# Norm factors and the scaling of the first banks issued first in a decoder trunk of twelve sub-layers

## The chip, the cores and the metric

One NeuronCore of one Trainium2 chip runs the whole program in one launch. The metric is the device time of that launch in microseconds (us). The engines are TensorE (PE, matrix products into PSUM banks), VectorE (DVE), ScalarE (ACT), GpSimd (POOL) and SyncE (SP, here the queue that issues nearly all loads). Each engine runs its own queue of instructions, and semaphores tie the queues together.

## The reference

A trunk of four layers on 256 tokens of width 1024 in 32-bit floats. Each layer is x += 1/2 gate SwiGLU(h), x += gate mixer(h), x += 1/2 gate SwiGLU(h), so there are twelve sub-layers. The mixers are differential attention in layers 0 and 3, RWKV-7 in layer 1 and sliding-window attention in layer 2. Ahead of each sub-layer stands the same norm with modulation:

```
def rms_norm(x, g, eps=NORM_EPS):
    y = xf * lax.rsqrt(jnp.mean(xf * xf, axis=-1, keepdims=True) + eps)
    return (y * g.astype(jnp.float32)).astype(x.dtype)

mod = (cond @ ada_w[i] + ada_b[i])[:, None, :]
h = modulate(rms_norm(x, norm_g[i, 0]), sh1, sc1)        # h * (1 + scale) + shift
x = x + 0.5 * g1 * swiglu(h, ffn_w_in[i, 0], ffn_w_out[i, 0])
```

Queries and keys in both attentions, the outputs of the differential heads and the keys and outputs of the RWKV heads are normed too.

## The kernel before

The activations lie transposed, as eight tiles of 128 features by 256 tokens. PE multiplies in a split form: each operand is a pair, a rounded part `hi` and the rest `lo`, and one product is three matmuls (`mm3`, lines 287 to 289: hi by hi, hi by lo, lo by hi). Weights come from memory as `raw` slabs of 1 MB; ACT makes `hi` (line 269) and DVE makes `lo` (line 271), four pieces of 512 columns each for a slab. The activations of a sub-layer are pairs from the pool `hp` (tag `h`, 10 tiles).

**The order of work.** The program text says what depends on what. A planner then lays the instructions of each engine in one queue: it plays the program through with its own estimates, and whenever an engine is free it takes, among the instructions that are ready at that moment, the one that stands first in the program. A load is asked for some units before its use, so the casts of later weights stand early in the text. Each tile takes one of the buffers of its tag and waits while none is free.

**A norm.** `residual` (line 577) makes a new tile of x. `stat_add` squares it, and one matmul with ones sums the squares. `rsqrt` turns the sums into the factor by bit arithmetic and two steps of refinement: a transpose (393), one affine step (402), nine tiny DVE steps on 128 x 8 elements (409 and 411 to 418), and a transpose back (424). Each needs the one before. With `later=True` it returns the last transpose as a function `fin`, to be called when the caller wants it.

**The start of a sub-layer.** While the factor is not known, PE already multiplies the raw x: `pre` makes a pair `xh` of x times (1 + scale) times the norm's gain (lines 489 and 490), with the shift as two extra columns. `first_units` runs the first products on these pairs into banks a, d and b of a feed-forward sub-layer (a, b and c in a mixer). `make_h` then makes the eight true `h` pairs: `xr` (511, DVE), the hi part (513, ACT), the lo part (514, DVE). The first banks are put right afterwards by `unraw`: ACT copies the extra column (540), and DVE multiplies the bank by the factor (541), which is the last read of that bank but for the copy, so that the bank comes free. In the text `unraw` stands behind `make_h`. In a feed-forward sub-layer the next products on `h` go to bank d and bank a again. Loads of the second pair of column blocks stand behind `make_h` in the text, and the products for later modulation vectors (`ada_unit`, line 344, DVE) from the third pair on.

**The mixers.** A differential head norms query and key (`qknorm`) and later its output (line 947 and after); an RWKV tile norms the key (at line 1252) and its output (at line 1429), and lines 1441 to 1443 use the latter factor; line 1443 is the last read of a bank d that line 1391 of the next tile needs. These calls of `rsqrt` use `later=True`, with pauses between the two halves in which other heads or tiles are stepped. `split` makes pairs of the `h` tag in the RWKV layer.

Of the kernel before, what the change touches and what calls it, by code (L numbers as in the profile page):

```python
# [16 lines left out]
ALU = mybir.AluOpType  # L17
# [4 lines left out]
T = 256  # L22
# [206 lines left out]
class Trunk:  # L229
    def __init__(self, tc, ctx, aps, plan):  # L230
        self.tc, self.nc, self.A, self.plan = tc, tc.nc, aps, plan
        e = ctx.enter_context
        self.cst = e(tc.tile_pool(name="cst", bufs=1))
        self.xp = e(tc.tile_pool(name="xp", bufs=9))
        self.sm = e(tc.tile_pool(name="sm", bufs=2))
        self.nrm = e(tc.tile_pool(name="nrm", bufs=2))
        self.hp = e(tc.tile_pool(name="hp", bufs=10))
        self.sl = e(tc.tile_pool(name="sl", bufs=4))
        self.pp = e(tc.tile_pool(name="pp", bufs=2, space=bass.MemoryType.PSUM))
        self.adp = None  # L240
        self.uid = 0
# [140 lines left out]
        return self.mods[(l, m)]  # L382


    def rsqrt(self, ps, n, scale, eps, pool, floor=None, later=False, more=None):


        nc = self.nc
        w, nk = n * 32, n
        n += 0 if more is None else more.shape[1]  # L390
        if nk:
            t = pool.tile([P, w], F32, tag=f"rsq{nk}", name=self.n("rsqt"))
            nc.vector.transpose(t, ps)
        m_ = self.sm.tile([P, n], F32, tag=f"rm{n}", bufs=3, name=self.n("rm"))
        m = m_[:, :nk]
        if more is not None:
            nc.vector.tensor_scalar(m_[:, nk:], more, scale, eps, op0=ALU.mult, op1=ALU.add)
        g = nc.vector
        if nk:
            first = t.rearrange("p (j q) -> p j q", q=32)[:, :, 0]  # L400
            if floor is None:
                g.tensor_scalar(m, first, scale, eps, op0=ALU.mult, op1=ALU.add)
            else:
                g.tensor_scalar(m, first, scale, floor, op0=ALU.mult, op1=ALU.max)
        m = m_
        y = self.sm.tile([P, n], F32, tag=f"ry{n}", bufs=3, name=self.n("ry"))
        z = self.sm.tile([P, n], F32, tag=f"ru{n}", bufs=3, name=self.n("rz"))
        f = self.sm.tile([P, n], F32, tag=f"rf{n}", bufs=3, name=self.n("rf"))
        g.tensor_scalar(y.bitcast(I32), m.bitcast(I32), -0.5, float(0x5f3759df), op0=ALU.mult, op1=ALU.add)

        g.tensor_tensor(z, y, y, op=ALU.mult)
        g.tensor_tensor(z, z, m, op=ALU.mult)
        g.scalar_tensor_tensor(y, z, -3.0, y, op0=ALU.add, op1=ALU.mult)
        g.tensor_tensor(z, y, y, op=ALU.mult)
        g.tensor_tensor(z, z, m, op=ALU.mult)
        g.tensor_scalar(f, z, -0.1875 / 16, 0.625 / 4, op0=ALU.mult, op1=ALU.add)
        g.tensor_tensor(f, f, z, op=ALU.mult)
        g.scalar_tensor_tensor(y, f, -0.9375, y, op0=ALU.add, op1=ALU.mult)

        def fin():  # L420
            if not nk:
                return None, y
            r = pool.tile([P, w], F32, tag=f"rsq{nk}", name=self.n("rsq"))
            nc.vector.transpose(r, y[:, :nk].unsqueeze(2).to_broadcast([P, nk, 32]))
            return r if more is None else (r, y[:, nk:])

        return fin if later else fin()

    def stat_begin(self):
        self.ssum = None  # L430
# [105 lines left out]
    def unraw(self, bank, out, tag="ub"):  # L536

        nc = self.nc
        b = self.sm.tile([P, 1], F32, tag=tag, bufs=4, name=self.n(tag))
        nc.scalar.copy(b, bank[:, T:T + 1])  # L540
        nc.vector.tensor_tensor(out, bank[:, :T], self.rs, op=ALU.mult)  # L541
        return b

    def split(self, pool, tag, bufs, src, sbuf=True):
# [566 lines left out]
    def rwkv(self, l):  # L1111
        nc, A = self.nc, self.A
        self.t1 = 4
        with ExitStack() as c0:
# [8 lines left out]
            with ExitStack() as c:  # L1123
# [21 lines left out]
                def mixed(i, d):  # L1145
                    t = ap.tile([P, T], F32, tag="mix", bufs=4, name=self.n("mix"))
                    om = omu[:, i * 8 + d:i * 8 + d + 1]
                    if i < 3:
                        nc.scalar.activation(t, pt[:, d, 1:], AF.Identity, scale=om, bias=sh[:, d:d + 1])
                    else:  # L1150
                        nc.gpsimd.tensor_scalar(t, pt[:, d, 1:], om, sh[:, d:d + 1], op0=ALU.mult, op1=ALU.add)
                    nc.vector.scalar_tensor_tensor(t, pt[:, d, :T], self.v("mu", i * 8 + d), t, op0=ALU.mult,
                                                   op1=ALU.add)
                    return t

                rkv = []
                for i in range(3):
                    ms = []
                    for d in range(ND):
                        if i == 0:  # L1160
                            nc.vector.scalar_tensor_tensor(pt[:, d, 1:], self.x[d], a[:, d:d + 1], r, op0=ALU.mult,
                                                           op1=ALU.mult)
                        ms.append(self.split(self.hp, "h", 10, mixed(i, d)))
                    if i == 2:
                        break
                    dst = self.slab(("hi", "lo")[i], (P, ND, T))
                    rkv.append(dst)
                    for u in range(4):
                        w = unit(i * 4 + u)
                        bank = self.ps("a" if u % 2 == 0 else "d")  # L1170
                        self.project(w, 2, ms, [bank[:, :T], bank[:, T:]], korder=(u < 2))
                        nc.scalar.copy(dst[:, 2 * u:2 * u + 2], bank.rearrange("p (d t) -> p d t", d=2))
                        self.pump(l, 20)
                    if i == 0:
                        l1 = self.slab("raw")
                        nc.sync.dma_start(l1, A["rwl1"])
                        l1b = ap.tile([P, T], F32, name=self.n("l1b"))
                        nc.sync.dma_start(l1b, A["rwl1b"])
                        nc.sync.dma_start(lw2[:, 0], A["rwl2"][0:128, :])
                        nc.sync.dma_start(lw2[:, 1], A["rwl2"][128:256, :])  # L1180
                        nc.sync.dma_start(lw2[:, 2], A["rwl2"][256:384, :])
                        l1 = l1.rearrange("p (k c) -> p k c", k=ND)
                        l1b = l1b.rearrange("p (k c) -> p k c", k=ND)
                        pl = [self.ps("c"), self.ps("c"), self.ps("b"), self.ps("b")]
                        for d in range(ND):
                            f = dict(start=(d == 0), stop=(d == ND - 1))
                            m = mixed(3, d)
                            nc.tensor.matmul(pl[0][0:64, :T], l1[:, d, 0:64], m, **f)
                            m = mixed(4, d)
                            nc.tensor.matmul(pl[1][64:128, :T], l1[:, d, 64:128], m, **f)  # L1190
                            m = mixed(5, d)
                            nc.tensor.matmul(pl[2][:, :T], l1[:, d, 128:256], m, **f)
                            nc.tensor.matmul(pl[3][0:32, :T], l1b[:, d], m, **f)
                        nc.scalar.activation(lr[0:64, 0], pl[0][0:64, :T], AF.Tanh)
                        nc.scalar.copy(lr[64:128, 1], pl[1][64:128, :T])
                        nc.scalar.activation(lr[:, 2], pl[2][:, :T], AF.Tanh, scale=0.5)
                        nc.vector.tensor_scalar(lr[:, 2], lr[:, 2], 0.5, 0.5, op0=ALU.mult, op1=ALU.add)
                        nc.scalar.activation(lr[0:32, 3], pl[3][0:32, :T], AF.Tanh, scale=0.5)
                        nc.vector.tensor_scalar(lr[0:32, 3], lr[0:32, 3], 0.5, 0.5, op0=ALU.mult, op1=ALU.add)
# [3 lines left out]
    def rw_core(self, c, l, rkv, lw2, lr, hw, ms, unit):  # L1203
# [3 lines left out]
        nc, A = self.nc, self.A  # L1207
# [10 lines left out]
        outs = []  # L1218
# [9 lines left out]
        def tile_gen(d):  # L1228
# [25 lines left out]
            fin = self.rsqrt(st[:, :T], 8, 64.0, 0.0, bp, floor=1e-24, later=True)  # L1254
# [49 lines left out]
            for h in range(2):  # L1304
                nc.vector.tensor_tensor(zb[hd[h]], zu[hd[h], :, h, 0], id64[hd[h]].unsqueeze(1).to_broadcast([64, 4, 64]),
                                        op=ALU.add)
# [21 lines left out]
            b = [self.ps(inv), self.ps(inv)]  # L1328
# [38 lines left out]
            for t in range(2):  # L1367
                for hh in range(2):
                    for h in range(2):
                        i, u = t * 2 + hh, hh * 2 + t  # L1370
# [46 lines left out]
            oo = f1("oo", 2)  # L1417
# [12 lines left out]
            fin = self.rsqrt(pv[:, :T], 8, 1.0, 64e-5, bp, later=True)  # L1430
# [10 lines left out]
            nc.vector.scalar_tensor_tensor(oo, oo, self.v("lnxg", d), rn, op0=ALU.mult, op1=ALU.mult)  # L1441
            nc.vector.scalar_tensor_tensor(oo, oo, self.v("lnxb", d), tt, op0=ALU.add, op1=ALU.add)
            nc.vector.tensor_tensor(oo, oo, pb[:, T:], op=ALU.mult)
            outs.append(self.split(self.hp, "h", 10, oo))

        rkv.append(self.slab("raw", (P, ND, T)))

# [67 lines left out]
```

## Time and profile before

| what | value |
|---|---|
| median of 3 runs | 2309.99 us (2307.81 to 2311.01) |
| the profiled execution | 2310.26 us, its span 2308.4 us |
| PE busy | 2193.9 us (95%) |
| DVE busy | 1766.9 us (77%) |
| ACT busy | 1196.4 us (52%) |
| mean granted TensorE clock | 0.974 |

The span runs from the first to the last instruction of the program; 1.9 us of the profiled execution lie around it. Busy time counts an instruction from start to end, so neighbours on DVE overlap by up to a tenth of a microsecond. [...]

### The profile page before, as it was taken

To read this page: it belongs to the slowest core of one execution; us is meant where nothing else is said; L and a number is where in the kernel's file an instruction comes from. 1 tells how busy PE (TensorE), PEld (TensorE's weight loads), DVE (VectorE), ACT (ScalarE), POOL (GpSimd) and SP (SyncE) were. 2 spreads that over 40 slices of the span, in tenths; PEclk is the share of its full clock that TensorE was granted. 3 is DMA by queue.
4 is the path that set the end of the run, shared out by engine and by line. 5 is a ranking of instruction groups with operands and counts; after the bars stand their busy time and mean duration, and the time that the engine had idled before them with its cause. 6 is when DMAs were issued, how large, how long until landed. Compare 5 with 4: busy or idle time off the path is not lost.

```text
span 2308.4 us, 47699 instructions
## 1 busy us (share of the span) xinstructions
PE 2193.9 (95%) x19244; PEld 2104.0 (91%) x19244; DVE 1766.9 (77%) x4001; ACT 1196.4 (52%) x2675; POOL 112.7 (5%) x213
## 2 busy tenths in 40 slices
PE   7999899999999899888999999999999999999999
PEld 6999898999999687677999899888999999889999
DVE  6877999888855776767888965778889855999653
ACT  3545766445444474445444644586445444766442
POOL 0001001001000300001000100101001000101000
PEclk8999999999999998899999999999999999999999
DMA  8885456887754420026788665436888755554552
GB/s 341 357 330 207 176 190 243 341 328 289 277 183 183 148 74 2 21 74 239 285 317 329 261 249 183 157 146 231 338 321 305 282 183 183 185 190 158 201 183 74
DMA packets 72365, 505.90 MB, mean 219 GB/s; under 512 B 8016, under 2 KB 10448, under 8 KB 11600
## 3 DMA queue, kind: packets, MB, share of 16 engines
q1 hardware_dynamic: 71568, 502.20, 57.6%
q8 instruction: 151, 2.47, 0.4%
q10 hardware_dynamic: 576, 0.66, 0.1%
q14 instruction: 70, 0.57, 0.1%
HBM read 501.78 MB, written 1.05 MB: 218 GB/s over the span
## 4 chain that ended last, share of the span: by engine, by line
PE 45%; DVE 5%; ACT 1%; issue 1%; POOL 0%; DVEq 0%; ACTq 0%; POOLq 0%
PE psa L287 4%; PE psa L289 4%; PE psa L288 4%; PE psd L287 4%; PE psd L289 4%; PE psd L288 4%; PE psb L288 3%; PE psb L287 3%; PE psb L289 3%; PE psc L288 2%; PE psc L289 2%; PE psc L287 2%; DVE lo L271 2%; DVE x L577 1%; DVE xh L490 1%
## 5 line engine op out<-in xcount | busy, mean ns | idle before, releaser
L269 ACT CAST hi<-raw 128x512 fp32r<-128x512 f32 x1306 | 731.3, 618 | 720.2 <-issue 553.5
L271 DVE TENSOR_TENSOR lo<-raw,hi 128x512 fp32r<-128x512 f32 x1306 | 847.3, 691 | 240.2 <-ACT hi L269 239.3
L287 PE MATMUL psa<-h,hi 128*128 128x256 f32 x1336 | 377.7, 283 | 29.3 <-DVE sil L541 23.8
L289 PE MATMUL psa<-h,lo 128*128 128x256 f32 x1336 | 377.3, 282 | 0.0
L288 PE MATMUL psa<-h,hi 128*128 128x256 f32 x1336 | 376.8, 282 | 0.0
L287 PE MATMUL psd<-h,hi 128*128 128x256 f32 x1256 | 359.0, 286 | 0.0
L289 PE MATMUL psd<-h,lo 128*128 128x256 f32 x1256 | 359.0, 286 | 0.0
L288 PE MATMUL psd<-h,hi 128*128 128x256 f32 x1256 | 358.4, 285 | 0.0
L344 DVE SCALAR_TENSOR_TENSOR ada<-ada,cb 128x1024 f32<-128x1024 f32 x232 | 276.3, 1219 | 27.1 <-DMA ada<-in_ada_dram 27.1
L287 PEld LDWEIGHTS psa<-h,hi 128*128 128x128 f32 x1336 | 255.0, 191 | 31.1 <-ACT hi L269 17.3
L288 PEld LDWEIGHTS psa<-h,hi 128*128 128x128 f32 x1336 | 253.0, 189 | 0.2
L289 PEld LDWEIGHTS psa<-h,lo 128*128 128x128 f32 x1336 | 252.9, 189 | 0.0
L287 PEld LDWEIGHTS psd<-h,hi 128*128 128x128 f32 x1256 | 243.7, 194 | 0.7
L288 PEld LDWEIGHTS psd<-h,hi 128*128 128x128 f32 x1256 | 242.4, 193 | 0.7 <-issue 0.7
L289 PEld LDWEIGHTS psd<-h,lo 128*128 128x128 f32 x1256 | 242.0, 193 | 0.3
L289 PE MATMUL psb<-g,lo 128*128 128x256 f32 x704 | 199.3, 283 | 0.0
L287 PE MATMUL psb<-g,hi 128*128 128x256 f32 x704 | 199.3, 283 | 0.0
L288 PE MATMUL psb<-g,hi 128*128 128x256 f32 x704 | 199.2, 283 | 0.0
L288 PE MATMUL psc<-g,hi 128*128 128x256 f32 x704 | 199.0, 283 | 0.0
L289 PE MATMUL psc<-g,lo 128*128 128x256 f32 x704 | 199.0, 283 | 0.0
L287 PE MATMUL psc<-g,hi 128*128 128x256 f32 x704 | 198.9, 283 | 0.0
L289 PEld LDWEIGHTS psb<-g,lo 128*128 128x128 f32 x704 | 135.0, 192 | 0.0
(373 smaller groups left out, 4464.4 us busy)
## 6 DMA issues: line engine op xcount, KB each, us to landing
raw<-in_ffi_dram SPq DMA_DIRECT2D x175, 1024.0 KB, 4.9
ada<-in_ada_dram SPq DMA_DIRECT2D x116, 1024.0 KB, 7.3
raw<-in_ffo_dram SPq DMA_DIRECT2D x88, 1024.0 KB, 4.9
raw<-in_ada_dram SPq DMA_DIRECT2D x24, 1024.0 KB, 4.8
raw<-in_daqk_dram SPq DMA_DIRECT2D x16, 1024.0 KB, 4.8
raw<-in_rwr_dram SPq DMA_DIRECT2D x12, 1024.0 KB, 4.8
raw<-in_ff_dram SPq DMA_DIRECT2D x8, 1024.0 KB, 9.6
raw<-in_dav_dram SPq DMA_DIRECT2D x8, 1024.0 KB, 4.8
```

The source lines that it names most:

```text
L269: nc.scalar.copy(hi[:, sl], raw[:, sl])
L271: eng.tensor_tensor(lo[:, sl], raw[:, sl], hi[:, sl].bitcast(F32), op=ALU.subtract)
L287: nc.tensor.matmul(out, whi, ahi, start=start, stop=False, skip_group_check=True)
L288: nc.tensor.matmul(out, whi, alo, start=False, stop=False, skip_group_check=True)
L289: nc.tensor.matmul(out, wlo, ahi, start=False, stop=stop, skip_group_check=True)
L344: nc.vector.scalar_tensor_tensor(wk, wk, 1.0, self.cond, op0=ALU.mult, op1=ALU.mult, accum_out=raw[:, k:k + 1])
L490: nc.vector.scalar_tensor_tensor(h[:, 1, :T], self.x[d], a[:, d:d + 1], h[:, 0, :T].bitcast(F32), op0=ALU.mult, op1=ALU.subtract)
L577: nc.vector.scalar_tensor_tensor(t, acc[d // 2][:, (d % 2) * T:(d % 2 + 1) * T], gate[:, d:d + 1], self.x[d], op0=ALU.mult, op1=ALU.add)
```

## The change

`rsqrt` becomes a wrapper around the old body, now `_rsqrt`. Both halves, the steps down to line 418 and the transpose back, are traced inside `high_priority()`, which makes the planner treat the instructions traced inside as if they stood at the start of the program. The same is done to the two instructions of `unraw`. Dependences are as they were, and no instruction is added or removed. The pool `hp` gets 12 tiles in place of 10.

```
-        self.hp = e(tc.tile_pool(name="hp", bufs=10))
+        self.hp = e(tc.tile_pool(name="hp", bufs=12))
...
-    def rsqrt(self, ps, n, scale, eps, pool, floor=None, later=False, more=None):
+    def rsqrt(self, *args, later=False, **kw):
+
+        with self.tc.high_priority():
+            fin = self._rsqrt(*args, **kw)
+
+        def done():
+            with self.tc.high_priority():
+                return fin()
+
+        return done if later else done()
+
+    def _rsqrt(self, ps, n, scale, eps, pool, floor=None, more=None):
...
-        return fin if later else fin()
+        return fin
...
-        nc.scalar.copy(b, bank[:, T:T + 1])
-        nc.vector.tensor_tensor(out, bank[:, :T], self.rs, op=ALU.mult)
+        with self.tc.high_priority():
+            nc.scalar.copy(b, bank[:, T:T + 1])
+            nc.vector.tensor_tensor(out, bank[:, :T], self.rs, op=ALU.mult)
...
-                        ms.append(self.split(self.hp, "h", 10, mixed(i, d)))
+                        ms.append(self.split(self.hp, "h", 12, mixed(i, d)))
...
-            outs.append(self.split(self.hp, "h", 10, oo))
+            outs.append(self.split(self.hp, "h", 12, oo))
```

## Rows read from the trace of the kernel before

**Rows 1.** The page, part 1: busy us, share, instructions.

```profile
PE 2193.9 (95%) x19244; PEld 2104.0 (91%) x19244; DVE 1766.9 (77%) x4001; ACT 1196.4 (52%) x2675; POOL 112.7 (5%) x213
```

**Rows 2.** Waits of PE: us in total, times, longest us.

```profile
PE psa L287 <- DVE sil L541: 23.8, 6, 4.5
...
PE psa L776 <- DVE qk L541: 6.0, 2, 3.5
...
PE psd L1391 <- DVE oo L1443: 5.1, 5, 1.0
...
PE psa L776 <- ACT hi L269: 4.7, 2, 3.8
```

**Rows 3.** Windows of 12 us: PE, PEld, DVE, ACT, POOL busy (instructions), PEclk, DMA.

```profile
380.27:392.27 12.00, 8.33 (x59) 8.36 (x60) 11.07 (x26) 7.94 (x17) 0.00 (x0) 0.86 0.33 125
...
1791.27:1803.27 12.00, 7.96 (x48) 7.95 (x49) 12.00 (x26) 6.62 (x16) 0.00 (x0) 0.72 0.31 116
2132.81:2144.81 12.00, 12.00 (x103) 12.00 (x103) 12.00 (x25) 8.99 (x21) 0.00 (x0) 1.00 0.30 96
```

**Rows 4.** Timeline of DVE at one late start: start us, us, line, operation.

```profile
1779.04 0.43 DVE L393 STREAM_TRANSPOSE rsqt<-psc 128x256 f32<-128x256 f32 x1
...
1780.69 0.16 DVE L409 TENSOR_SCALAR ry<-rm 128x8 int32<-128x8 int32 x1
1780.76 0.68 DVE L271 TENSOR_TENSOR lo<-raw,hi 128x512 fp32r<-128x512 f32 x1
...
1782.12 1.22 DVE L344 SCALAR_TENSOR_TENSOR ada<-ada,cb 128x1024 f32<-128x1024 f32 x1
...
1787.20 0.16 DVE L418 SCALAR_TENSOR_TENSOR ry<-rf,ry 128x8 f32<-128x8 f32 x1
...
1787.88 0.43 DVE L424 STREAM_TRANSPOSE rsq<-ry 128x256 f32<-128x256 f32 x1
...
1788.81 1.27 DVE L511 SCALAR_TENSOR_TENSOR xr<-x,mod,rsq 128x256 f32<-128x256 f32 x3
...
1794.75 0.41 DVE L541 TENSOR_TENSOR sil<-psa,rsq 128x256 f32<-128x256 f32 x1
```

**Rows 5.** Timeline of DVE at the undisturbed start.

```profile
2126.50 0.44 DVE L424 STREAM_TRANSPOSE rsq<-ry 128x256 f32<-128x256 f32 x1
...
2130.59 0.42 DVE L541 TENSOR_TENSOR sil<-psa,rsq 128x256 f32<-128x256 f32 x1
```

**Rows 6.** Timeline of DVE where nothing else was ready (layer 0's mixer).

```profile
229.91 0.17 DVE L409 TENSOR_SCALAR ry<-rm 128x8 int32<-128x8 int32 x1
...
231.53 0.17 DVE L418 SCALAR_TENSOR_TENSOR ry<-rf,ry 128x8 f32<-128x8 f32 x1
```

**Rows 7.** Groups by line: count, busy us, mean ns, idle before and its releasers.

```profile
L513 ACT ACTIVATE h<-xr,mod 128x256 fp32r<-128x256 f32 x80 | 35.7, 501 | 15.6 <-DVE xr L511 13.8 <-PE psc L289 1.1 <-PE psb L289 0.3
...
L409 DVE TENSOR_SCALAR ry<-rm 128x8 int32<-128x8 int32 (+2 forms) x64 | 10.6, 166 | 0.5
```

**Rows 8.** Timeline of ACT at another late start.

```profile
1596.72 1.28 ACT L651 ACT_TABLE_LOAD   x1
1598.01 0.91 ACT L651 ACTIVATE sil<-sil,ub 128x256 f32<-128x256 f32 x2
```

**Rows 9.** Windows, columns as in rows 3: RWKV tiles, differential heads, steady feed-forward.

```profile
843.00:1066.00 223.00, 200.40 (x3342) 161.32 (x3340) 154.92 (x509) 106.40 (x338) 1.25 (x8) 0.92 0.15 55
252.00:354.00 102.00, 98.63 (x738) 93.31 (x737) 95.33 (x364) 69.92 (x189) 4.29 (x11) 0.98 0.52 192
...
1605.00:1755.00 150.00, 150.00 (x1264) 150.00 (x1263) 124.79 (x213) 67.47 (x126) 0.32 (x2) 1.00 0.86 329
```

**Rows 10.** Timeline of DVE in the RWKV layer.

```profile
897.28 0.16 DVE L418 SCALAR_TENSOR_TENSOR ry<-rf,ry 128x8 f32<-128x8 f32 x1
...
903.29 0.76 DVE L424 STREAM_TRANSPOSE rsq<-ry 128x256 f32<-128x256 f32 x2
...
905.74 0.41 DVE L1443 TENSOR_TENSOR oo<-oo,psd 128x256 f32<-128x256 f32 x1
```

## The prediction

> **What bounds the kernel now.** I read the page first, then the waits of TensorE (PE), then time windows at each place where PE waits, and last the order of VectorE's (DVE) queue at those places. [...] The waits of PE name the largest single cause [rows 2]: six times, for 23.8 us together, PE waits for line 541, the `unraw` multiply that scales a first bank of a feed-forward sub-layer by the norm factor and so frees the bank. Two more waits for line 541 (6.0 us) and two booked to a cast (4.7 us) lie at the starts of the mixers, and behind most of them is the same multiply. Five waits of 1.0 us each in the RWKV layer are for line 1443.
>
> The six starts cost more than the waits. In the 12 us after PE's last matmul on raw input, the one undisturbed start of a feed-forward sub-layer executes 103 matmuls at clock 1.00; the six others execute 59, 50, 43, 54, 46 and 48 [rows 3], which show the first and the last of the six and the undisturbed one. That is 300 where 618 would fit: 318 missing, at 12/103 = 0.1165 us each, or 37.0 us. The granted clock in those windows is 0.72 to 0.86, so the rest above 23.8 is matmuls at half clock after each wait.
>
> Why line 541 is late is seen in DVE's queue at one of the six [rows 4]. The twelve steps of the norm factor, ten of them tiny, take from 1779.04 to 1788.31, because between every two of them one large instruction runs, a `lo` cast or an `ada` product. After the factor, DVE makes `h` tiles, and only at 1794.75 comes the first multiply of line 541; PE had run out of raw work at 1791.27, where its window in [rows 3] begins. At the undisturbed start [rows 5] the factor comes at 2126.94 and line 541 at 2130.59, before PE runs out of raw work.
>
> **The change, part by part.** *The factor's steps go first.* Does that take the large instructions out from between them? I say no. The `ada` product at 1782.12 stands behind the norm in the program (it is issued from the third pair on, the norm in the first pair), and it was placed in the middle of the chain all the same. So these instructions did not win by order: they filled the moment in which the next step was not ready. A dependent step starts 0.20 us after the one before it, though nothing else runs (1.62 us for eight steps) [rows 6], and a step occupies less. First place changes nothing there. I cost this part at 0 and expect the chain at the six starts to stay near 6.5 us between lines 409 and 418; if it shrank to 1.62, that would be worth 4.9 us of lead (a rival, below).
>
> *The multiplies of line 541 go first.* They need only the factor and a full bank, so the four of banks a and d move from behind the `h` tiles to right behind the factor. At the start of [rows 4]: factor at 1788.31, one fill until 1788.81, four multiplies at a pitch of 0.33 us until 1790.15, then `xr` 0.40 us, ScalarE's half of `h` 0.50 us [rows 7], DVE's half about as long as `xr`: first `h` at 1791.5. Where the Silu of the first bank, now ready earlier, gets in front of `h` with a table load as in [rows 8] (I allow for three of the six starts), 0.5 us later. PE, out of raw work at 1791.27, would wait 0.3 to 0.8 us instead of 4.0. From there it is paced by DVE, which needs 0.80 us for the two instructions of each `h`, against six matmuls or 0.70 us: 0.8 us over eight. With 0.5 us for what half clock may remain, each start keeps about 2 us, all six 12. Gain 37 - 12 = 25 us. Bounds: 37, if nothing remains; and if each start keeps 1.5 us of waiting and all its half clock (windows at 0.72 four times and 0.86 twice lack 16.8 us of full clock in all), 37 - 9 - 16.8 = 11.
>
> A table load is 1.28 us in the trace, and the Silu starts 1.29 us after the load did [rows 8]; that is what the 0.5 us above rests on. [...]
>
> *The mixers' starts.* The same move. The waits there are 6.0 + 4.7 = 10.7 us [rows 2]. In the two differential layers the pool counts as well: with 10 tiles, eight hold the raw input, so the third `h` waits until PE has done with the first of them; line 513 shows 1.1 us of waiting for PE [rows 7], and it would be more once the factor is not late. I take 8 us: about three quarters, as the `h` tiles keep DVE busy till the same time as before. Bounds 0 and 14 (10.7 and the half clock of two such starts).
>
> *The pool* itself only adds room; no instruction is added or removed by it. Nor do the moved steps issue a DMA or stand in SP's or POOL's queue. At the six starts it does nothing: when the factor comes, PE has released nearly all raw tiles. What the multiplies delay at the starts is `lo` casts for later weights; PE waits for none of them in the steady part, where it is busy 150.00 of 150 us with DVE at 124.79 [rows 9].
>
> *The factors inside the mixers* (52 of the 64 chains; 12 are those of the sub-layers' norms [rows 7]). In the RWKV layer the second half, the transpose of line 424, is issued at 903.29, though its input was ready at 897.44, and line 1443, which PE waits for, follows at 905.74 [rows 10]. First place could bring the transpose forward by up to 5.8 us and take away the five waits, 5.1 us, and part of the half clock that the layer shows (223 us at 0.92, so 17.8 us lacking at most [rows 9]). But DVE had moments without work between 897 and 903 and did not take it, so something else than order, such as the free buffers, may hold it. Bounds 0 and 23; I take 4, nearer to 0 for that reason.
>
> **The sum** is made against the profiled execution, 2310.26 us (0.27 above the median shown): 2310.26 - 25 - 8 - 4 = 2273 us. About 0.2% is what a measurement of this kernel can tell from no change, 4.6 us.
>
> **The rivals.** *The chain gets tight.* If first place does keep the large instructions out, the factor comes 4.9 us sooner at the six starts, line 541 and all `h` are done before PE needs them as in [rows 5], and the 37 us go entirely. With 10 at the mixers, 4 in RWKV and 2 for its last tile's chain: 2310.3 - 53 = 2257. Against it: the `ada` product in the chain. Chance 0.15.
>
> *The wait changes its name.* PE waits for `h` instead of for line 541, since the multiplies take DVE time that `h` needs; and the two multiplies of the third pair of banks, if queued right behind the first four, hold DVE until PE has finished those banks, from 1790.15 to about 1791.3, with all `h` behind them. DVE runs its queue in order, as everything in [rows 4] does. [...] Then the starts give only their lower bound 11, the mixers 3, RWKV nothing: 2296. Chance 0.17.
>
> *The change doesn't do what it says.* The multiplies of line 541 are held by something else than order, the slots of `sil` and `gf`, say, and everything stays within 0.2%: 2310. For it: the transpose at 903.29. Against: sub-layer starts have fresh buffers. Chance 0.05.
>
> *Slower.* In the differential layers DVE is busy 95.33 of 102 us [rows 9], so whatever goes first there pushes something else back, and that is `lo` casts of the next weights. If each of the 16 heads made one unit's four casts late for PE (4 x 0.68 = 2.7 us), that is 43 us, 6 more than the gain: 2316. It decides from 2.3 us for each head on (37/16). Against it: four units are loaded ahead. Chance 0.05.
>
> **The numbers.** The forecast has 0.58, its own range 2260 to 2286. Faster by over 0.2% are the forecast and the first two rivals, 0.90; same 0.05; slower 0.05. The range takes in the tight chain and the renamed wait and stops short of the last two: 2250 to 2297.
>
> **What would show it.** Right: line 541 directly behind line 424 at all six starts; the 541 entry of PE's waits nearly gone; 85 or more matmuls in the 12 us windows, clock above 0.9; `ada` and `lo` still between the steps. Wrong: a chain of 1.6 us at the starts (first rival), or a new entry of 10 us or more in which PE waits for `h` (second). RWKV is tested by line 424 following line 418 within 1 us, and by the five waits. The prediction fails most easily in the clock: a wait of 1 us may bring the same half clock as one of 4.

## The result, and the profile after

The changed kernel takes 2272.19 us (median of 4 runs, 2271.19 to 2272.90), the kernel before in the same comparison 2310.50 us (2307.81 to 2313.37): ratio 0.9834, 95% interval 0.9817 to 0.9851. The forecast was 2273. The profiled execution of the changed kernel took 2271.19 us, its span is 2269.1 us, 39.3 us shorter than that of before.

Lines from the factor on are 11 higher now, those from the multiply on 12 higher: the factor's steps run from line 404 to line 429, its closing transpose is line 435, the multiply of `unraw` line 553, the RWKV line that PE waits for line 1455.

The page's part 1 of the changed kernel, as in [rows 1]:

```profile
PE 2178.7 (96%) x19244; PEld 2089.3 (92%) x19244; DVE 1757.3 (77%) x4001; ACT 1193.7 (53%) x2675; POOL 117.7 (5%) x213
```

The table cuts both profiled executions at the end of the eighth addition to `x` of each layer part (line 577 before, 589 after), which is where each part hands over to the next. The granted clock is the PEclk of the profile: the share of full speed that PE was given, as a mean over the stretch. Two stretches of before, the first at the fifth of the six late starts, the second at the undisturbed one (columns as in [rows 3]):

```profile
1597.00:1602.00 5.00, 5.00 (x24) 5.00 (x24) 4.98 (x12) 3.53 (x8) 0.00 (x0) 0.50 0.34 103
...
2133.00:2138.00 5.00, 5.00 (x45) 5.00 (x44) 5.00 (x13) 4.99 (x14) 0.00 (x0) 1.00 0.00 0
```

PE is busy for the whole of both and executes 24 matmuls at 0.50 and 45 at 1.00. So in the table the clock below 1.00 is weighed as time lost: a microsecond at 0.50 counts as half of one.

| parts | before us | after us | clock lost, before and after | difference | in the sum of the prediction |
|---|---|---|---|---|---|
| six late feed-forward parts | 1185.7 | 1159.7 | 18.8, 3.4 | -26.0 | -25 |
| three attention mixers | 386.6 | 372.7 | 10.2, 3.4 | -13.9 | -8 |
| RWKV mixer | 323.5 | 325.3 | 23.9, 23.9 | +1.8 | -4 |
| first and last feed-forward part | 409.2 | 408.4 | 6.8, 6.8 | -0.8 | 0 |

Of the 39.3 us, 22.2 are clock (59.7 us lost before, 37.5 after). The total came out within 1 us of the forecast, and that is in part luck: the first row came out as forecast and for the reason given, but the second gained 5.9 us more than its term and the third, which was to gain 4, gained nothing. The two misses cancel.

Waits of PE in the changed kernel, columns as in [rows 2]:

```profile
PE psc L287 <- ACT o L561: 6.7, 2, 4.3
...
PE psd L1403 <- DVE oo L1455: 5.1, 5, 1.0
...
PE psd L288 <- DVE h L525: 3.9, 6, 0.8
```

The entry for line 541 (now 553), 23.8 us in [rows 2], is gone, and so are both entries at the mixers' starts. PE now waits six times for the second half of an `h` tile, 0.65 us each: this is the new name that the second rival spoke of, at a sixth of the old size. The wait for `o`, the output of the attention heads, has grown from 2.3 to 6.7 us. The five RWKV waits stand unchanged at 5.1 us.

Windows of 12 us behind PE's last matmul on raw input, columns as in [rows 3]; the first and the last of the six late starts, and the one that was undisturbed before:

```profile
376.25:388.25 12.00, 10.73 (x87) 10.40 (x87) 12.00 (x28) 10.20 (x24) 0.00 (x0) 1.00 0.37 137
...
1763.50:1775.50 12.00, 11.21 (x92) 10.93 (x92) 11.66 (x25) 8.89 (x19) 0.00 (x0) 1.00 0.18 67
2093.72:2105.72 12.00, 12.00 (x104) 12.00 (x103) 12.00 (x24) 8.64 (x20) 0.00 (x0) 1.00 0.29 96
```

The six hold 87, 92, 86, 91, 95 and 92 matmuls, 543 where 300 stood; 75 are missing of the 618, or 75 x 0.1165 = 8.7 us in place of 37.0. The clock is 1.00 in all of them.

VectorE's (DVE) timeline at the start that [rows 4] showed, columns as there:

```profile
1751.35 0.45 DVE L404 STREAM_TRANSPOSE rsqt<-psc 128x256 f32<-128x256 f32 x1 [0.39 <-PE psc L478]
...
1752.37 1.22 DVE L344 SCALAR_TENSOR_TENSOR ada<-ada,cb 128x1024 f32<-128x1024 f32 x1
...
1753.51 0.17 DVE L420 TENSOR_SCALAR ry<-rm 128x8 int32<-128x8 int32 x1
1753.59 0.68 DVE L271 TENSOR_TENSOR lo<-raw,hi 128x512 fp32r<-128x512 f32 x1
...
1758.94 0.16 DVE L429 SCALAR_TENSOR_TENSOR ry<-rf,ry 128x8 f32<-128x8 f32 x1
...
1759.62 0.43 DVE L435 STREAM_TRANSPOSE rsq<-ry 128x256 f32<-128x256 f32 x1
1759.98 0.65 DVE L271 TENSOR_TENSOR lo<-raw,hi 128x512 fp32r<-128x512 f32 x1
1760.55 0.41 DVE L553 TENSOR_TENSOR sil<-psa,rsq 128x256 f32<-128x256 f32 x1
...
1763.79 0.42 DVE L553 TENSOR_TENSOR sil<-psb,rsq 128x256 f32<-128x256 f32 x1 [0.31 <-ACT ub L552]
1764.13 1.27 DVE L525 SCALAR_TENSOR_TENSOR h<-xr,mod,h 128x256 fp32r<-128x256 f32 x3
```

The large instructions still stand between the steps, 5.4 us from line 420 to line 429 (6.5 before; at all six starts 5.4 to 6.0 us, 5.4 to 6.5 before). The first multiply follows 0.93 us behind the closing transpose where it took 6.87 us. Ahead of the last multiply DVE stands for 0.31 us behind ScalarE's copy from bank b (line 552), into which PE was still multiplying, and the `h` instructions stand behind it: the second rival's mechanism, at a third of a microsecond.

DVE in the RWKV mixer, the lines of [rows 10], and the mixer's window before and after (columns as in [rows 3]):

```profile
885.94 0.16 DVE L429 SCALAR_TENSOR_TENSOR ry<-rf,ry 128x8 f32<-128x8 f32 x1
...
892.13 0.76 DVE L435 STREAM_TRANSPOSE rsq<-ry 128x256 f32<-128x256 f32 x2
...
894.58 0.41 DVE L1455 TENSOR_TENSOR oo<-oo,psd 128x256 f32<-128x256 f32 x1
```
```profile
759.25:1082.77 323.52, 288.22 (x3940) 235.60 (x3939) 228.29 (x675) 159.81 (x456) 31.43 (x49) 0.93 0.23 84
```
```profile
746.83:1072.16 325.33, 288.48 (x3942) 235.49 (x3941) 227.27 (x675) 160.11 (x456) 31.12 (x49) 0.93 0.23 84
```

The transpose is issued 6.2 us behind the start of line 429, which makes its input (6.0 before), although it now has first place. Here first place did nothing.

### The profile page after: what moved, and what is told of

It is laid out like the page before. It is cut to its first block, busy times and chain, and to the rows that moved or that the text cites. A ratio compares the mean times of both kernels' runs of the same rounds, so it can differ in the third digit from the quotient of the medians.

```text
span 2269.1 us, 47573 instructions
## 1 busy us (share of the span) xinstructions
PE 2178.7 (96%) x19244; PEld 2089.3 (92%) x19244; DVE 1757.3 (77%) x4001; ACT 1193.7 (53%) x2675; POOL 117.7 (5%) x213
## 4 chain that ended last, share of the span: by engine, by line
PE 53%; DVE 7%; ACT 2%; issue 2%; DMA 1%; POOL 0%; DVEq 0%; ACTq 0%; POOLq 0%
PE psa L288 5%; PE psa L289 5%; PE psa L287 4%; PE psd L288 4%; PE psd L289 4%; PE psd L287 4%; PE psb L287 4%; PE psb L288 4%; PE psb L289 4%; PE psc L287 3%; PE psc L288 3%; PE psc L289 3%; DVE lo L271 2%; DVE xh L501 1%; DVE x L589 1%
## 5 line engine op out<-in xcount | busy, mean ns | idle before, releaser
L288 PE MATMUL psd<-h,hi 128*128 128x256 f32 x1256 | 355.4, 283 | 3.9 <-DVE h L525 3.9
L287 PE MATMUL psd<-h,hi 128*128 128x256 f32 x1256 | 353.8, 282 | 1.5 <-ACT ub L552 1.5
L288 PEld LDWEIGHTS psd<-h,hi 128*128 128x128 f32 x1256 | 236.8, 189 | 6.0 <-DVE h L525 5.2
L287 PEld LDWEIGHTS psd<-h,hi 128*128 128x128 f32 x1256 | 239.0, 190 | 2.6 <-ACT ub L552 1.9
L289 PEld LDWEIGHTS psd<-h,lo 128*128 128x128 f32 x1256 | 236.6, 188 | 0.3
L288 PEld LDWEIGHTS psb<-g,hi 128*128 128x128 f32 x704 | 135.3, 192 | 0.0
```

Of the source, the lines that this page charges most:

```text
L287: nc.tensor.matmul(out, whi, ahi, start=start, stop=False, skip_group_check=True)
L288: nc.tensor.matmul(out, whi, alo, start=False, stop=False, skip_group_check=True)
L289: nc.tensor.matmul(out, wlo, ahi, start=False, stop=stop, skip_group_check=True)
```

## The experiments

The main theory: at the six starts the gain is that of `unraw` going first; the factor's first place acts elsewhere; RWKV is held by something else than order. The rivals: the factor's place does the work, or the pool does. All medians below are of 4 runs (10 for `e2_factor` and `e3_pool`), each ratio is to the kernel before in the same series. The last table of this section cuts every profiled execution as above.

**The three edits one by one, and the two without the pool.** `e1_unraw` is the kernel before with only

```
+        with self.tc.high_priority():
             nc.scalar.copy(b, bank[:, T:T + 1])
             nc.vector.tensor_tensor(out, bank[:, :T], self.rs, op=ALU.mult)
```

> The kernel before with only the two instructions of the bank scaling (copy and multiply) put first; factor steps and pool of 10 as before. Theory A (the gain is the place of the multiply): the six late feed-forward starts lose their wait for the multiply and get 26 us faster together as in the changed kernel, the sliding-window start 3 to 4 us, the RWKV layer stays within 1 us; in all 2274 to 2284 us. Rival B (the factor's first place carries the gain): 2295 us or more, with at least half of the 23.8 us of waits for the multiply left. Rival C (the larger pool is needed for the early multiply to pay): the six starts gain less than 13 us, since h tiles wait for PE to release raw tiles.

`e2_factor` is the changed kernel without that block and with the pool at 10:

> The kernel before with only the factor's steps put first; bank scaling and pool of 10 as before. Theory A: the ada and lo instructions still stand between the steps (5.4 to 6.5 us from the first to the last tiny step at the six starts), the wait of PE for the multiply stays at 22 to 25 us, the mixers move by at most 6 us either way, RWKV gets up to 2 us slower as the changed kernel did: 2303 to 2313 us. Rival B: 2295 us or less.

`e3_pool` is the kernel before with `bufs=12` in place of 10 at the three places of the diff:

> The kernel before with only the pool of 12 tiles. Theory A: the six starts are as before, since the factor comes after PE has released nearly all raw tiles; the two differential layers gain 0 to 3 us together: 2306 to 2312 us. Rival C: below 2300 us.

`e4_pool10` is the changed kernel with 10 there:

> The changed kernel with the pool back at 10 tiles. Theory A: the six starts within 0.5 us each of the changed kernel, the differential layers up to 4 us slower together: 2271 to 2278 us. Rival C: 2285 us or more.

Measured: `e1_unraw` 2286.25 us (0.9908, 0.9883 to 0.9934), `e2_factor` 2306.02 (0.9987, 0.9968 to 1.0006), `e3_pool` 2310.45 (1.0009, 0.9994 to 1.0024), `e4_pool10` 2270.92 (0.9842, 0.9813 to 0.9872). The pool does nothing that can be measured, alone or with the rest. At the six starts `unraw` alone gives -26.2 us, all that the change gives there. Its total lies 2 us above the expected range: the sliding layer, which was to gain 3 to 4 us, has 100.9 us against 99.8, and RWKV lost 29.0 us of clock. It stops 14 us short of the changed kernel, and the factor alone gives 2.7 in its series, which its interval does not tell from nothing: the two are worth more together than apart, and not at the six starts. Alone, neither makes the attention mixers shorter (388.3 and 390.7 us against 386.6; `e12_before_tag`, which edits the RWKV layer alone, has 388.8 there); together they make them 372.7 (373.9 with 10 tiles). The first differential layer before, with `unraw` alone, with the factor alone and with both (columns as in [rows 3]):

```profile
222.80:366.10 143.30, 134.23 (x988) 127.17 (x988) 130.67 (x451) 97.27 (x255) 14.01 (x27) 0.96 0.52 188
222.43:369.37 146.94, 136.25 (x988) 127.48 (x988) 131.97 (x450) 97.22 (x255) 14.74 (x27) 0.94 0.50 184
222.86:367.26 144.40, 133.57 (x988) 126.27 (x988) 130.88 (x450) 97.82 (x255) 12.62 (x27) 0.98 0.51 186
221.87:362.00 140.13, 133.76 (x985) 126.18 (x986) 128.42 (x450) 96.64 (x254) 15.06 (x27) 0.98 0.52 189
```

The stretch less PE's busy time is what PE stands still: 9.1, 10.7, 10.8 and 6.4 us. The waits of PE in this layer with `unraw` alone:

```profile
PE psa L777 <- ACT s L921: 3.1, 3, 2.2
PE psa L778 <- DVE kn L912: 2.6, 1, 2.6
```

Lines 777 and 778 are the scores of a head, which need the key scaled by the head's own factor (`kn`; 1.5 us of waiting before) and the bank that the softmax of another head must first read (`s`). This reads as if PE, with the raw banks out of the way early, comes to the scores before the head's factor is ready. With the factor alone, the waits for the multiply remain:

```profile
PE psa L287 <- DVE sil L552: 20.2, 6, 4.5
...
PE psa L787 <- DVE qk L552: 6.1, 2, 3.5
```

Its six starts are 8.7 us shorter than before, but 8.6 of that is clock.

**Where the factor's place acts.** Two kernels test that reading. `e8_heads` is the changed kernel in which only the heads' factors are first:

```
-    def rsqrt(self, *args, later=False, **kw):
+    def rsqrt(self, *args, later=False, early=False, **kw):
+        if not early:
+            fin = self._rsqrt(*args, **kw)
+            return fin if later else fin()
```

with `early=True` in the calls of lines 828 and 960.

> The changed kernel, with the factor's steps first only for the norms inside the heads of the attention mixers (queries and keys, and the differential heads' outputs); the factor of each layer part's own norm and both RWKV factors take their turn as in the kernel before. unraw stays first everywhere. Theory: at the six feed-forward starts unraw alone is the gain, and the factor's first place acts in the heads: total 2268 to 2276, the six starts still 24 to 27 us below before, the three attention mixers 12 to 15 below. Rival: the first place counts for the layer norm's own factor at the mixers' starts: three mixers as with unraw alone (388 us together instead of 372.7), total 2282 to 2289.

`e11_ff_unraw` is `e1_unraw` with the block only in the three calls of `ffn()`; in the heads `unraw` takes its turn:

> The kernel before, with unraw's two instructions first in the feed-forward layers alone; in the attention heads they take their turn, the factor takes its turn everywhere, pool of 10. Theory: the heads lose where unraw is first and the factor is not, since PE then reaches the scores before the head's factor is there; without it the mixers stand as before and the six starts keep their 26 us: 2280 to 2285, first differential layer 142 to 144.5 us (146.9 with unraw first in the heads too), sliding layer 99 to 101. Rival: the mixers' loss with unraw alone came from the six starts (weights and casts that now come in another phase): first differential layer 146 to 148, total 2285 to 2289.

`e8_heads` took 2274.97 us (0.9852, 0.9829 to 0.9874): six starts -24.9, attention mixers -12.8, as the theory had it. `e11_ff_unraw` took 2283.50 (0.9881, 0.9866 to 0.9896): the six starts keep -23.9, the first differential layer is at 143.29 us and the sliding layer at 99.94, against 143.30 and 99.78 before, and the wait of [rows 2] is back at its old size:

```profile
PE psa L777 <- DVE qk L542: 6.0, 2, 3.5
```

The last differential layer has 145.5 us (143.6 before, 140.4 in `e1_unraw`), so the three mixers together stand at 388.7, as in `e1_unraw` (388.3). Without the heads' factors first, an early `unraw` in the heads is thus worth nothing; that it does harm there, as the theory had it, is not shown, since the first differential layer alone, 146.9 us in `e1_unraw`, reaches 145.8 in `e12_before_tag`, where nothing in it was edited. So the mixers' gain belongs to the pair "first banks early, and the heads' factors early behind them"; the factors of the layer norms need no first place. Not run: the heads' factors first with `unraw` first in the feed-forward parts alone.

**RWKV: a tag of its own.** The two 256-wide tiles of a factor share one tag with those of the next key norm. `e5_tag` is the changed kernel with another tag for the output norm's tiles:

```
-            t = pool.tile([P, w], F32, tag=f"rsq{nk}", name=self.n("rsqt"))
+            t = pool.tile([P, w], F32, tag=f"rsq{nk}{tg}", name=self.n("rsqt"))
...
-            fin = self.rsqrt(pv[:, :T], 8, 1.0, 64e-5, bp, later=True)
+            fin = self.rsqrt(pv[:, :T], 8, 1.0, 64e-5, bp, later=True, tg="g")
```

and the same for the second tile.

> The changed kernel, with one more edit: in the RWKV mixer the two tiles of the output norm's factor get a tag of their own instead of sharing the tag of the key norm's. Theory: tiles of one tag are given out in the order of the text, so the output norm's last transpose (line 435) waits for a tile that the next key norm must take first, whatever stands first in the queue; with its own tag it goes right behind line 429. Then the five waits of line 1403 for line 1455 (5.1 us) go, and part of the mixer's half clock with them: RWKV stage 325.3 to 315 to 321 us, total 2262 to 2268. Rival: another input of line 1403, or the key norm that is now pushed back, takes the wait over: stage within 2 us of 325, total 2270 to 2274.

`e12_before_tag` is the kernel before with this edit alone, so with nothing first:

> The kernel before, with nothing but the own tag for the RWKV output norm's factor. Theory: the order in which tiles of one tag are given out held line 424 of the output norm, and no first place is needed to free it: the five waits of line 1391 for line 1443 go, RWKV stage 3 to 8 us below 323.5, total 2302 to 2307. Rival: without a first place the transpose and the three steps behind it wait for their turn anyway: 2309 to 2312.

`e5_tag` took 2262.73 us (0.9789, 0.9763 to 0.9814). DVE there, on the tile shown above:

```profile
885.51 0.15 DVE L429 SCALAR_TENSOR_TENSOR ry<-rf,ry 128x8 f32<-128x8 f32 x1
...
885.78 0.43 DVE L435 STREAM_TRANSPOSE rsq<-ry 128x256 f32<-128x256 f32 x1
...
891.98 0.41 DVE L1455 TENSOR_TENSOR oo<-oo,psd 128x256 f32<-128x256 f32 x1
```

The transpose follows 0.27 us behind the start of line 429. The entry of line 1403 is gone from the waits, and in its place stands another, which was 1.7 us in the changed kernel:

```profile
PE psd L1394 <- DVE wuv L1387: 6.6, 6, 1.2
```

So the expectation and its rival were each half right: the wait changed its name, and yet the mixer is 7.7 us shorter. `e12_before_tag` took 2294.50 us (0.9932, 0.9911 to 0.9953), 17 us under before in its series where 3 to 8 had been expected. There too line 424 follows 0.27 us behind the start of line 418, and the wait moved to the line of `wuv` (6.3 us). Its mixer, columns as in [rows 3]:

```profile
761.60:1067.96 306.36, 271.37 (x3941) 223.93 (x3940) 227.35 (x675) 158.77 (x456) 31.24 (x49) 0.97 0.24 89
```

It is 17.2 us shorter than before, 0.97 in place of 0.93 of the clock; of the difference 23.9 - 10.2 = 13.7 us is clock given back and 3.5 the rest. No first place was needed. PE stands still for as long as before, 35.0 us against 35.3 (stretch less busy time), so what the tag gave here is not less waiting. In `e5_tag`, on the other hand, the mixer lost 25.6 us of clock, more than the 23.9 of the changed kernel, and PE stands still for 2.9 us less. That the tag shortens the kernel is shown by the medians; by what way is open. Why the clock falls in this mixer by 10.2 us in one execution and by 17.1 to 29.0 in others is not settled.

**The chain without anything between its steps.** `e7_tight` tests the first rival of the prediction: the changed kernel with the casts and products of pairs 1 to 3 tied behind the closing transpose (`self.end` is what line 435 issues):

```
+                hold = ExitStack()
+                if hs and not first and j < 4:
+                    hold.enter_context(self.tc.issue_after(self.end.ins))
                 if j < NPAIR:
                     wg, wu = (self.load(A["ffi"][(base + j) * 2 + f]) for f in range(2))
...
                     self.ada(k)
+                    hold.close()
```

> The changed kernel, with the weight casts and modulation products of pairs 1 to 3 queued behind the last step of the feed-forward's norm chain (line 435), so that none of them stands between two steps. Main account: the chain at the six starts falls from 5.4 to 6.0 us to 1.7 to 2.7 us, but only 8.2 us of loss are left at these starts in the changed kernel, so it gains 3 to 8 us: total 2264 to 2269. Rival 1 of the prediction (a tight chain is worth 13 us more): 2257 to 2261. Second rival (the casts pushed back make the up weights of pair 1 late, and PE waits for line 271 instead): 2274 to 2290, with PE entries on lo.

`e9_once` takes work out at the same place: behind the first pair, `ffn()` loads the gate weights of pair 1 a second time, and nothing reads them.

```
-                    wg, wu = (self.load(A["ffi"][(base + j) * 2 + f]) for f in range(2))
+                    wg, wu = (None if j == 1 and ahead and f == 0 else self.load(A["ffi"][(base + j) * 2 + f]) for f in range(2))
```

> The changed kernel without a transfer that nothing reads: behind the first pair ffn() loads the gate weights of pair 1 a second time (7 feed-forward layers, 1 MB, four casts on ScalarE and four on VectorE each). Those four VectorE casts are among the work that stands between the chain's steps at the six starts. If work between the steps costs what it takes at its face (four casts of about 0.6 us at seven starts), 14 to 17 us go: 2255 to 2258. Main account: PE has the raw products as cover, and what is left to win is the 8.2 us of loss at the starts and some of the transfer time behind them: 2262 to 2270. Rival: nothing of it is on the path: 2270 to 2274.

`e7_tight` took 2262.79 us (0.9796, 0.9778 to 0.9814), between its first two expectations and 9.4 us under the changed kernel. Its profiled execution took 2272.40, 1.2 us over that of the changed kernel, so the gain of the other runs is not in this trace. Its mean granted clock is 0.981, that of the other three 0.985 and 0.986, which is some 10 us less lost, as much as they are shorter; the changed kernel's four runs had 0.983 to 0.985, so a part of the 9.4 us is clock. The chain is what it should be, 3.0 us from line 404 to the end of line 435 at each of the six starts. In this execution PE got nothing for it there: the six windows hold 73, 87, 74, 88, 86 and 88 matmuls, 496 against 543, and the start that was undisturbed holds 86 against 104. In the place of `h` it waits for the next weights and for the last multiply, both pushed back; the first of the six:

```profile
PE psa L287 <- ACT hi L269: 0.7, 1, 0.7
PE psb L287 <- DVE sil L553: 0.7, 1, 0.7
```

`e9_once` took 2270.36 us (0.9833, 0.9816 to 0.9850), no gain: its third expectation. Its six windows hold 67, 85, 81, 86, 103 and 84, 506. The chain did not get shorter by the casts that went: from line 404 to the end of line 435 it takes 9.8 to 10.3 us at five of the six starts, where the changed kernel has 8.7 to 9.2, so other ready instructions took their place between the steps.

**Both, and all.** `e10_tag_tight` joins the edits of `e5_tag` and `e7_tight`, `e13_three` those and `e9_once`.

> The changed kernel with both edits that took about 9 us each: the own tag for the RWKV output norm's factor, and the casts of pairs 1 to 3 behind line 435. The two touch different layer parts, so their gains should add: 2272.2 - 9.5 - 9.4 = 2253, range 2249 to 2257. Rival: the gains are two readings of one thing, how long the clock stays halved in the RWKV layer, and don't add: 2259 to 2264. At the six starts the chain (line 404 to line 435) should be near 3 us; if the gain of the tight chain lies at the starts, these feed-forward parts are 1 to 2 us shorter each than after the change alone.

> As e10_tag_tight, and the gate weights of pair 1 loaded once instead of twice. With no work between the chain's steps, the casts that the unread transfer brings stand right behind the chain, ahead of the up weights of pair 1, for which PE now waits a little: four casts of about 0.6 us on VectorE and a transfer of 4.9 us less at each start. Theory: 0.5 to 1 us at each of seven starts: 4 to 7 us below e10_tag_tight. Rival: these waits are 0.7 us at most, and nothing else there is on the path: within 2 us of it.

`e10_tag_tight` took 2256.70 us (0.9771, 0.9741 to 0.9800), inside the first expectation, but its interval overlaps that of `e5_tag`, so that the gains add is not shown; its six windows hold 520. `e13_three` took 2235.17 us (0.9670, 0.9649 to 0.9691): 75 us under the kernel before, 21.5 under `e10_tag_tight` where 4 to 7 were expected. Its page, part 1, and two of its six windows:

```profile
PE 2160.8 (97%) x19244; PEld 2078.8 (93%) x19244; DVE 1743.9 (78%) x3973; ACT 1171.8 (52%) x2647; POOL 116.2 (5%) x213
```
```profile
376.71:388.71 12.00, 12.00 (x102) 12.00 (x102) 12.00 (x22) 7.83 (x18) 0.00 (x0) 1.00 0.70 263
567.29:579.29 12.00, 12.00 (x104) 12.00 (x103) 12.00 (x23) 6.40 (x15) 0.00 (x0) 1.00 0.70 263
```

The six hold 616 of 618, PE does not wait in them, and the six parts are 11.5 us shorter than in `e10_tag_tight`. In these traces the tight chain shortens the six parts by much only where the casts that it pushes back are not late themselves, and dropping the unread load (28 instructions fewer on DVE and on ScalarE) does so only behind a tight chain. The profiled executions differ by 12 us at the same granted clock, 0.986; the medians differ by 21.5. The other 9.5 lie in runs without a trace, and their clock differs: 0.987 to 0.991 in the other three of `e13_three`, 0.981 and 0.982 in two of `e10_tag_tight`.

| profiled execution | us | six late starts | attention mixers | RWKV (clock lost) | first and last part |
|---|---|---|---|---|---|
| before | 2310.26 | 1185.7 | 386.6 | 323.5 (23.9) | 409.2 |
| changed | 2271.19 | 1159.7 | 372.7 | 325.3 (23.9) | 408.4 |
| e1_unraw | 2289.40 | 1159.5 | 388.3 | 327.5 (29.0) | 408.9 |
| e2_factor | 2306.59 | 1177.0 | 390.7 | 324.1 (23.9) | 409.3 |
| e3_pool | 2314.78 | 1184.8 | 388.9 | 324.4 (27.3) | 411.6 |
| e4_pool10 | 2272.17 | 1159.6 | 373.9 | 324.9 (25.6) | 408.5 |
| e8_heads | 2270.35 | 1160.8 | 373.8 | 321.6 (20.5) | 409.1 |
| e11_ff_unraw | 2286.11 | 1161.8 | 388.7 | 322.1 (22.2) | 408.4 |
| e5_tag | 2264.22 | 1159.8 | 373.5 | 317.6 (25.6) | 408.1 |
| e12_before_tag | 2295.01 | 1186.6 | 388.8 | 306.4 (10.2) | 408.2 |
| e7_tight | 2272.40 | 1160.3 | 370.1 | 320.6 (22.2) | 416.2 |
| e9_once | 2273.55 | 1161.0 | 373.6 | 325.4 (25.6) | 408.5 |
| e10_tag_tight | 2252.39 | 1156.6 | 368.3 | 309.0 (17.1) | 413.4 |
| e13_three | 2240.44 | 1145.1 | 368.0 | 312.2 (20.5) | 410.1 |

## Why the prediction was right, point by point

**The six starts: right, and shown.** 26.0 us against 25, and `e1_unraw` has them from the multiply's place alone. The chain kept its `ada` and `lo`, as forecast. The step that was named as the weakest, the clock, went better than feared: no window fell below 1.00, so each start kept 8.7/6 = 1.45 us instead of 2. The table loads allowed for came at three of the six starts, as here on ScalarE at the first (columns as in [rows 8]):

```profile
374.74 1.28 ACT L663 ACT_TABLE_LOAD   x1 [2.10 <-DVE sil L553]
376.03 0.51 ACT L663 ACTIVATE sil<-sil,ub 128x256 f32<-128x256 f32 x1
```

The Silu starts 1.29 us behind the load's start again.

**The mixers: right in sign, mis-sized, and only half understood.** The term was 8 us, "the same move" as at the six starts. It measured 13.9, of which 6.8 are clock, at its upper bound of 14. What it left out is that a head has a factor of its own between the multiply and PE's next work: without the heads' factors first, the same move brought these layers nothing (388.3 us against 386.6). "First place changes nothing there" held for the six starts, for which it was said; in the heads, with the banks early, it does not hold. These layers vary by some 2 us where no edit touches them (386.6 to 388.8), so 1 or 2 us mean nothing there; but all eight kernels with both edits lie between 368.0 and 373.9, and none without the pair lies under 386.6, so that the two work together is shown. That PE came to the scores too early is argued from the waits.

**RWKV: the step failed, for the reason kept beside it.** The prediction took 4 us and said that something else than order, such as the free buffers, may hold line 424. It was held, and by the tag: with a tag of its own the transpose follows at once, in `e5_tag` and in `e12_before_tag`. That the order of the text is the reason (the key norm's tiles stand between the output norm's two) and not the number of buffers is not shown, since a tag of its own brings buffers of its own as well. So the 4 us had nothing under them: first place alone gave this mixer +1.8 us, within what it varies by. The upper bound of 23 us was nearer to what lay there: with the tag alone on the kernel before, 17 us came, in the profiled execution mostly as clock.

**The rivals.** A wait with a new name came (3.9 us for `h`) but at a sixth of the old one, so its case of 2296 did not. The tight chain did not arise by itself; when it was made, PE's loss at the starts moved to the weights, and a gain of the size that this rival put there (12 us more than the forecast) came only with the unread load gone: the six parts are 14.6 us shorter in `e13_three` than after the change, 3.1 in `e10_tag_tight`. The pool: nothing, as costed. The slower case, late `lo` casts in the differential heads, does not show: these layers became shorter.

## What to carry to other kernels

Look at what the engine that waits will need next before giving one instruction first place: here the early multiply paid at once where only the `h` tiles lay behind it, and brought nothing where a second chain lay behind it that had no first place. First place moves an instruction only among those that are ready; it neither closes the gaps of a dependent chain nor frees a tile, so a transpose that starts 6 us late while its engine has time to spare points to what it must be given, not to its rank. An edit that measures as nothing alone (the unread load dropped: 2270.36 us against 2272.19) was worth 12 us in the profiled executions behind a tight chain, so a list of single edits does not tell what their sum does.

## What the runs showed of the hardware

At one place the granted clock differs where PE's work does not. `e7_tight` and `e10_tag_tight` have the same instructions at the first of the six starts and the same waits (0.7 and 0.7 us, named above), and PE stands still for the same 1.40 us in the 12 us window. PE's longest wait for `o` is 4.3 us in either kernel; in the changed kernel it is the only wait in the 40 us ahead of this start. The first of the next two lines is `e7_tight`, the second `e10_tag_tight` (columns as in [rows 3]):

```profile
380.19:392.19 12.00, 10.60 (x73) 10.12 (x73) 10.42 (x19) 7.45 (x16) 0.00 (x0) 0.86 0.67 264
```
```profile
375.85:387.85 12.00, 10.60 (x85) 10.12 (x85) 11.94 (x22) 8.96 (x19) 0.00 (x0) 1.00 0.70 263
```

One was granted 0.86 of the clock, the other all of it: 73 matmuls against 85, 12 fewer, or 1.4 us by estimate (12 x 0.1165 us), for nothing that PE did differently here. Why is not shown.

Runs of one kernel differ too. `e5_tag` ran from 2253.01 to 2264.22 us, and the mean granted clock was 0.989 in the first and 0.983 in the second, which is by estimate (span times the missing share) some 14 us of clock lost more, enough for the difference. Where in the slower run it was lost is not known, as the quick one left no trace.
